# First loads, MLP entry and the end of the RWKV stage rearranged, RWKV preparation in fixed turns of two row halves

## The chip, the cores and the metric

The kernel runs on one core of one Trainium2 chip. The metric is the device time of one execution in microseconds (us). Three runs of the kernel before took 4267.73, 4275.2 and 4288.86 us, median 4275.2 us.

## The reference, cut to what matters

One inference step of a backbone of two layers on 1280 tokens (256 of a prompt, 1024 of a sample) of width 1024. Layer 0 mixes tokens with a gated DeltaNet beside a short convolution, layer 1 with windowed attention beside RWKV-7; each layer ends in an MLP of width 4096.

```python
for layer in range(2):
    mod = silu(c) @ mod_w[layer] + mod_b[layer]        # shift, scale, gate, twice; c_ctx for the prompt
    h = rmsnorm(x, norm_mix) * (1 + mod[1]) + mod[0]
    x = x + mod[2] * (even_mixer(h) if layer == 0 else odd_mixer(h))
    h = rmsnorm(x, norm_mlp) * (1 + mod[4]) + mod[3]
    x = x + mod[5] * (square(relu(h @ mlp_w1)) @ mlp_w2)
y = rmsnorm(x, norm_final)

def rwkv7_mixer(x):                                     # 8 heads of 64, both directions
    r, k, v, wl, al, gl = split(token_shift_bi(x, mu))
    decay = exp(-exp(-softplus(-(w0 + tanh(wl) @ w_up)) - 0.5))   # low rank 64, per direction
    a = sigmoid(a0 + al @ a_up)                                   # low rank 64, per direction
    kk = l2norm(k * k_k);  k2 = k * (1 + (a - 1) * k_a)
    y = scan(S = S*decay - (S kk)(kk*a)^T + v k2^T;  y = S r)     # forward + backward
    y = groupnorm(y) * ln_w + ln_b + sum(r * k2 * r_k) * v        # bonus
    return y * (sigmoid(gl) @ g_up)                               # gate
odd_mixer(h) = concat(attention(h), rwkv7_mixer(h)) @ w_out
```

## The kernel before, in words

Tokens stand along the free dimension and features on the 128 partitions: x is eight tiles of 128 x 1280. A dense product is exact to fp32 by three products of split operands (`split`, L245: hi = rounded copy on ACT, lo = src - hi on POOL or DVE; `dense_mm`, L270). The tokens are worked in chunks of 512, 512 and 256. A scheduler sets the order on each engine by a simulated time line; helpers steer it (`behind` and `late` put one instruction behind another, `chain` gives time to the serial work and `paced` spends it on dense work between).

Start (L1881 to L1898): x is loaded in five pieces of 1 MB on ACT's queue and transposed, the conditions c and c_ctx come on SP's queue (`load_vec(1)`, L196), two sets of modulation weights on SP's queue feed PE (`mod_set`, L297, products at L305), and the norm makes the first dense operands. `spill_x` (L124, store at L126) writes x out, 8 stores of 640 KB on SP's queue.

Even mixer (L590 on): `qkv(0, 1)`, then a product of 32 columns for beta and a (L711, L712), then `qkv(0, 0)`, `qkv(0, 2)`, `z_gate(0)`. Between the chunks `go_on(3)` issues three steps of the next modulation: ACT scales a weight tile (L357), POOL adds it up (L361). The squares of q and k are ACT's L630, their column sums PE's L635.

The first MLP starts behind a norm (L448, L455 on DVE). The modulation of layer 1 is made on DVE here (L348 and L350 in `mod_vec`), one step behind each eviction of the MLP's output (L512).

RWKV (L1298 on) runs in 8 units: 4 pairs of heads x 2 directions. A unit has five groups of 256 tokens, 40 groups in all. `prep` (L1524) makes a group's operands: two low-rank products (L1548) in one bank of `pp` (two banks), read by ACT (L1550); four Gram matmuls for each head (L1588), read by DVE (L1590); four transposes for each head (L1595), read by ACT (L1597). A head is a half of the 64 + 64 rows of the array. `recur` runs the serial chunks and alternates the halves matmul by matmul (L1698, L1713 and others). Dense products of the odd projection (L1276) and then attention fill PE between. `finish(b)` (L1797) ends a pair of heads after its second direction in five parts: load r and k (tile `vg`, one buffer), head norm, transposes L1827, bonus L1829, gate L1835, store to `sp_w` (L1838). For the first three pairs the parts run inside the next unit; for the last pair they run after unit 7.

`odd_out` (L1844): `unspill_x` loads x on ACT's queue in 24 pieces (L131); eight operands of 640 KB are loaded through two buffers on alternating queues (L1849) and split; `project` (L1861) multiplies them by od_w_out, 4 + 4 column blocks, and adds into x (L1866). Then come the norm, the second MLP and the final norm.

Of the kernel before, what the change touches and what calls it, by code (L numbers as in the profile page):

```python
# [85 lines left out]
def tile_kernel(ctx, tc, I, O):  # L86
# [37 lines left out]
    def spill_x(xt):  # L124
        for kb in range(KB):
            SY.dma_start(out=x_dram[kb], in_=xt[kb])  # L126
# [69 lines left out]
    load_vec(1, SY, const)  # L196

# [11 lines left out]
    def behind(bi, other):  # L209
        tc.add_manual_dep(bi.ins, other.ins.name, mybir.DependencyInfo(mybir.DependencyClass.NoSync, mybir.DependencyReason.DATA),  # L210
                          reason="one sum at a time in a bank")
# [77 lines left out]
    V.memset(scp, 0.0)  # L289
    for s, nm in enumerate(("c_ctx", "c")):  # L290
        th = cvec[:, s, :]
        A.activation(out=th, in_=vec[nm], func=AF.Tanh, scale=0.5)
        V.scalar_tensor_tensor(out=th, in0=th, scalar=1.0, in1=vec[nm], op0=ALU.add, op1=ALU.mult)
        V.tensor_scalar(out=scp[:, :, s], in0=th, scalar1=0.5, scalar2=None, op0=ALU.mult)
    mods = [const.tile([P, 48, 2], F32, name=f"mods{l}") for l in range(2)]

    def mod_set(wp, l, u):  # L297

        ps = ps_t("pm")
        for kb in range(KB):  # L300
            for j in range(2):
                w = wp.tile([P, 512], F32, tag="modw", name="modw")
                c0 = u * D + 512 * j
                SY.dma_start(out=w, in_=I["mod_w"][l, kb * P:(kb + 1) * P, c0:c0 + 512])
# [31 lines left out]
    def mod_vec(wp, ring, bank, l, c0, n, on_v, loads=None):  # L336
# [4 lines left out]
        for kb in range(KB):  # L341
            src = I["mod_w"][l, kb * P:(kb + 1) * P, c0:c0 + n]
            if on_v:
                w = state[ring].tile([P, n], F32, tag=ring, name="modw")
                SY.dma_start(out=w, in_=src)
                for s in range(2):
                    if kb == 0:
                        V.tensor_scalar(out=acc[:, s], in0=w, scalar1=scp[:, kb, s:s + 1], scalar2=None, op0=ALU.mult)  # L348
                    else:
                        V.scalar_tensor_tensor(out=acc[:, s], in0=w, scalar=scp[:, kb, s:s + 1], in1=acc[:, s],  # L350
                                               op0=ALU.mult, op1=ALU.add)
# [126 lines left out]
    def mlp(es, l, xt, hs, gate, side=()):  # L478
# [7 lines left out]
        for g in range(FF // 256):  # L486
# [16 lines left out]
            def down(hid, t0, N, s):  # L503
                hh, hl = hid
                for db in range(KB):
                    ps = ps_m()
                    for b in range(2):
# [4 lines left out]
                    V.scalar_tensor_tensor(out=xt[db][:, t0:t0 + N], in0=ps[:, :N],  # L512
                                           scalar=gate[:, db, s:s + 1], in1=xt[db][:, t0:t0 + N],
                                           op0=ALU.mult, op1=ALU.add)
# [66 lines left out]
    def even_mixer(hs):  # L581
# [9 lines left out]
        with ExitStack() as es:  # L591
# [19 lines left out]
            def qkv(h, i):  # L611
# [5 lines left out]
                for t0, N, s in CHUNKS:  # L617
# [4 lines left out]
                    go_on(3)  # L622
# [19 lines left out]
            def z_gate(j):  # L642
                hl = load_w(w_cols(wi, 1536 + j * P))
                zt_ = cp.tile([P, T], F32, tag="cv", name="zg", bufs=2)
                for t0, N, s in CHUNKS:
# [5 lines left out]
                    go_on(3)  # L651
# [4 lines left out]
            def short_conv(j, i):  # L656
# [5 lines left out]
                for t0, N, s in CHUNKS:  # L662
# [10 lines left out]
                    go_on(3)  # L673
# [18 lines left out]
            steps = mod_steps()  # L692
# [10 lines left out]
            hl = state["whl"].tile([P, KB, 2, 16], F32R, tag="whl", name="whl")  # L703
# [47 lines left out]
            for i in (0, 2):  # L751
                qkv(0, i)
# [324 lines left out]
    def odd_mixer(xt, hs, hes, xes, wes):  # L1077
# [20 lines left out]
        mid.update(a=sp_a, w=sp_w)  # L1098
# [53 lines left out]
        with ExitStack() as es:  # L1152
# [37 lines left out]
            for j in (12, 13, 14):  # L1190
# [9 lines left out]
                SY.dma_start(out=(sp_l[0], sp_l[1], sp_g)[j - 12], in_=dst)  # L1200
# [98 lines left out]
        with ExitStack() as es:  # L1299
# [22 lines left out]
            for u, (b, d) in enumerate(units):  # L1322
# [11 lines left out]
                else:  # L1334
# [4 lines left out]
                    if u >= 7:  # L1339
                        pace["used"] = max(pace["used"], start - 0)  # L1340
# [7 lines left out]
                if d == 1:  # L1348
                    ends = finish(b)
            for f in ends:  # L1350
                f()
# [148 lines left out]
    def rwkv(es, sp_r, sp_v, sp_t, sp_l, sp_g, sp_k2):  # L1500
# [23 lines left out]
        def prep(b, d):  # L1524
# [3 lines left out]
            if d == 0:  # L1528
                ups = tp.tile([P, 3, P], F32, tag="ups", name="ups", bufs=2)
                for i, src in enumerate((I["rwkv_w_up"].rearrange("e d r c -> (e d r) c"),  # L1530
                                         I["rwkv_a_up"].rearrange("e d r c -> (e d r) c"), I["rwkv_g_up"][0])):
                    SY.dma_start(out=ups[:, i], in_=src[:, b * P:(b + 1) * P])
# [5 lines left out]
            for c0 in order:  # L1538
# [4 lines left out]
                lin = tp.tile([P, 2, 256], F32, tag="lin", name="lin", bufs=1)  # L1543
                SY.dma_start(out=lin[hr[d]], in_=sp_l.rearrange("x p t -> p x t")[hr[d], :, sl])
                ps = ps_t("pp")
                lt = tp.tile([P, 2, 256], F32, tag="lt", name="lt", bufs=2)
                for i in range(2):
                    chain(PE.matmul(ps[:, 256 * i:256 * i + 256], ups[hr[d], i, :], lin[hr[d], i, :],  # L1548
                                    start=True, stop=True), 0.43)
                    A.activation(out=lt[:, i], in_=ps[:, 256 * i:256 * i + 256], func=AF.Tanh, scale=0.5,  # L1550
# [24 lines left out]
                g = state["more"] if state["more"] and turn[0] % 11 in (1, 2, 3) else gp  # L1575
# [9 lines left out]
                for h in range(2):  # L1585
                    ps = ps_t("pp")
                    for c in range(4):
                        chain(PE.matmul(ps[:, P * c:P * c + P], BK[hr[h], c, h:h + 2, :].rearrange("p a q -> p (a q)"),  # L1588
                                        AR[hr[h], c].rearrange("p a q -> p (a q)"), start=True, stop=True), 0.22)
                    V.tensor_tensor(out=Gm[:, :, h, 64:], in0=ps.rearrange("p (c q) -> p c q", c=4),  # L1590
                                    in1=gmask[:, d, h:h + 1].to_broadcast([P, 4, P]), op=ALU.mult)
                for h in range(2):
                    ps = ps_t("pp")
                    for c in range(4):
                        chain(PE.transpose(ps[:, 64 * c:64 * c + 64], BK[hr[h], c, h:h + 2, :].rearrange("p a q -> p (a q)"),  # L1595
# [362 lines left out]
```

## Time and profile before

| | us |
|---|---|
| median of three runs | 4275.2 |
| profiled execution | 4277.4 |
| its span | 4275.4 |
| PE busy (92%) | 3933.8 |
| DVE busy (53%) | 2285.1 |
| ACT / POOL busy (30% each) | 1285.4 / 1300.8 |
| mean granted TensorE clock | 0.944 |

The span is 1.9 us shorter than the profiled execution's own time. Busy time counts an engine's instructions, not its waits; the granted clock is the share of full TensorE speed (1.0 is 2.4 GHz, 0.5 is 1.2 GHz). In a waits view, "line <- engine tile line" is the instruction that waited and what ended the wait. In a timeline the bracket is the idle time ahead of an instruction and what ended it, and `x16` are sixteen records that stand as one row. A matmul of fp32 operands has two records.

### The profile page before, as it was taken

Reading aid. Unit: us, or ns where it says so; the run is one execution under the profiler, and the core shown is the slowest. Engines: PE = TensorE matmul, PEld = TensorE weight load, DVE = VectorE, ACT = ScalarE, POOL = GpSimd, SP = SyncE. Lnnn points to the kernel's source line nnn. Section 1 sums busy time; section 2 is a strip of 40 time slices with the busy share of each in tenths; the row PEclk is TensorE's granted clock in tenths of the full one; section 3 lists DMA queues with packets and bytes.
Section 4 is the critical chain, followed back from the end, with each engine's and each line's share of the span. In section 5 each row is a group of like instructions: output and inputs, shape, how many; then the busy total and the mean of one; then the engine's idle time right before and its main releaser. Section 6 shows DMA issues by size and latency. Waiting matters only on the chain. (4 is left out here: it accounts for less than half of the span.)

```text
span 4275.4 us, 68726 instructions
## 1 busy us (share of the span) xinstructions
PE 3933.8 (92%) x27295; PEld 3228.1 (76%) x27295; DVE 2285.1 (53%) x4799; ACT 1285.4 (30%) x2721; POOL 1300.8 (30%) x1139
## 2 busy tenths in 40 slices
PE   6889989998999999999889889999868899999999
PEld 3677877786888888877667667777647788888887
DVE  5377676546455555463365577778541533333335
ACT  4454543223111111143222234444321311111112
POOL 2444542224222332242432231212022323322232
PEclk8889999999999999999989889999879999999999
DMA  5323332332122222125466543333242111111111
GB/s 206 101 81 100 93 98 70 126 131 73 53 75 72 71 79 75 47 98 181 147 211 185 137 101 82 91 88 82 64 134 67 30 40 40 40 35 35 40 40 60
DMA packets 437952, 382.90 MB, mean 90 GB/s; under 512 B 125684, under 2 KB 373503, under 8 KB 437503
## 3 DMA queue, kind: packets, MB, share of 16 engines
q1 hardware_dynamic: 405802, 314.45, 25.0%
q10 hardware_dynamic: 31829, 64.06, 4.5%
q8 instruction: 215, 3.52, 0.3%
q14 instruction: 106, 0.87, 0.1%
HBM read 290.31 MB, written 88.08 MB: 89 GB/s over the span
## 5 line engine op out<-in xcount | busy, mean ns | idle before, releaser
L275 PE MATMUL pd<-hhi,whl 128*128 128x512 f32 (+1 forms) x5376 | 1538.8, 366 | 55.0 <-ACT hhi L247 25.3
L275 PEld LDWEIGHTS pd<-hhi,whl 128*128 128x128 f32 x5376 | 974.9, 193 | 213.4 <-ACT hhi L247 27.1
L275 PE MATMUL pd<-hlo,whl 128*128 128x512 f32 (+1 forms) x2688 | 986.0, 367 | 27.1 <-POOL hlo L251 13.4
L512 DVE SCALAR_TENSOR_TENSOR x<-pm,mods,x 128x512 f32<-128x512 f32 (+1 forms) x768 | 501.7, 659 | 724.9 <-PE pm L511 724.7
L251 POOL TENSOR_TENSOR whl<-raw,whl 128x1024 fp32r<-128x1024 f32 (+1 forms) x203 | 471.2, 2331 | 611.3 <-ACT whl L247 610.1
L275 PEld LDWEIGHTS pd<-hlo,whl 128*128 128x128 f32 x2688 | 518.1, 193 | 115.3 <-DVE hlo L455 19.2
L509 PE MATMUL pm<-hh,whl 128*128 128x512 f32 (+1 forms) x1536 | 545.7, 356 | 0.0
L510 PE MATMUL pm<-hl,whl 128*128 128x512 f32 (+1 forms) x1536 | 544.4, 354 | 0.0
L511 PE MATMUL pm<-hh,whl 128*128 128x512 f32 (+1 forms) x1536 | 542.9, 354 | 0.0
L498 ACT ACTIVATE t<-pd 128x512 f32<-128x512 f32 (+1 forms) x192 | 101.1, 528 | 1307.6 <-PE pd L275 1305.3
L251 POOL TENSOR_TENSOR hl<-t,hh 128x512 fp32r<-128x512 f32 (+1 forms) x192 | 217.6, 1134 | 822.5 <-DVE hh L249 802.5
L509 PEld LDWEIGHTS pm<-hh,whl 128*128 128x128 f32 x1536 | 288.9, 188 | 44.5
L510 PEld LDWEIGHTS pm<-hl,whl 128*128 128x128 f32 x1536 | 289.4, 188 | 43.5
L511 PEld LDWEIGHTS pm<-hh,whl 128*128 128x128 f32 x1536 | 289.5, 188 | 41.7
L249 DVE CAST hh<-t 128x512 fp32r<-128x512 f32 (+1 forms) x192 | 164.0, 855 | 228.4 <-ACT t L499 228.3
L247 ACT ACTIVATE whl<-raw 128x1024 fp32r<-128x1024 f32 (+1 forms) x203 | 201.7, 1011 | 162.8 <-PE pm L511 74.7
L361 POOL TENSOR_TENSOR acc<-acc,modw 128x512 f32<-128x512 f32 x112 | 152.3, 1360 | 151.9 <-ACT modw L357 132.4
L357 ACT ACTIVATE modw<-modw,scp 128x256 f32<-128x256 f32 x224 | 113.0, 506 | 67.3 <-DMA modw<-in_mod_w_dram 61.9
L1276 PE MATMUL pa<-hst,whl 128*128 128x512 f32 (+1 forms) x432 | 121.1, 380 | 9.5 <-DMA hst<-sp_h 8.5
L350 DVE SCALAR_TENSOR_TENSOR acc<-modw,scp,acc 128x512 f32<-128x512 f32 x168 | 129.1, 800 | 0.2 <-DMA modw<-in_mod_w_dram 0.2
L284 PE MATMUL pd<-hhi,whl 128*128 128x512 f32 (+1 forms) x384 | 109.2, 364 | 4.9 <-ACT hhi L247 3.0
L420 ACT ACTIVATE sq<-x 128x512 f32<-128x512 f32 (+1 forms) x120 | 66.2, 558 | 157.3 <-DVE x L1866 48.0
(388 smaller groups left out, 5989.8 us busy)
## 6 DMA issues: line engine op xcount, KB each, us to landing
raw<-in_mlp_w_dram SPq DMA_DIRECT2D x128, 512.0 KB
modw<-in_mod_w_dram SPq DMA_DIRECT2D x128, 256.0 KB
hst<-sp_h ACTq DMA_DIRECT2D x48, 512.0 KB
modw<-in_mod_w_dram SPq DMA_DIRECT2D x128, 128.0 KB
rkk<-sp_r SPq DMA_DIRECT2D x40, 384.0 KB
raw<-in_ev_w_in_dram SPq DMA_DIRECT2D x28, 512.0 KB
x_dram<-x SPq DMA_DIRECT2D x16, 640.0 KB
x<-x_dram ACTq DMA_DIRECT2D x32, 256.0 KB
```

The source lines that it names most:

```text
L247: A.activation(out=hi, in_=src, func=AF.Copy)
L249: V.tensor_copy(out=hi, in_=src)
L251: G.tensor_tensor(out=lo, in0=src, in1=hi.bitcast(F32), op=ALU.subtract)
L275: paced(PE.matmul(ps[:, :N], w, x[:, t0:t0 + N], start=(n + i == 0), stop=(n == KB - 1 and i == 2)), N / 2400)
L350: V.scalar_tensor_tensor(out=acc[:, s], in0=w, scalar=scp[:, kb, s:s + 1], in1=acc[:, s], op0=ALU.mult, op1=ALU.add)
L357: bi = A.activation(out=dst[:, s], in_=w[:, 0], func=AF.Copy, scale=scp[:, kb, s:s + 1])
L361: G.tensor_tensor(out=acc, in0=acc, in1=w, op=ALU.add)
L509: PE.matmul(ps[:, :N], wh, hh[:, b, :N], start=(b == 0), stop=False)
L510: PE.matmul(ps[:, :N], wh, hl[:, b, :N], start=False, stop=False)
L511: PE.matmul(ps[:, :N], wl, hh[:, b, :N], start=False, stop=(b == 1))
L512: V.scalar_tensor_tensor(out=xt[db][:, t0:t0 + N], in0=ps[:, :N], scalar=gate[:, db, s:s + 1], in1=xt[db][:, t0:t0 + N], op0=ALU.mult, op1 ...
L1276: burst([(lambda w_=w_, i=i, w=w, h=h: PE.matmul(st["ps"][w_][:, :N], st["w"][w_][:, w, kb, :], x[:, h, :N], start=(kb + i == 0), stop=(kb ...
```

## The change

1. Start: the conditions are loaded on ACT's queue after the first two pieces of x (`conditions()`), the modulation weights come first on SP's queue, and the eight stores of x stand behind the last of them. 2. Even mixer: `qkv(0, 1)` and `qkv(0, 0)` come ahead of the beta and a product, which has tiles of its own; `go_on` begins at the tenth call with four steps each. 3. First MLP: DVE's modulation steps stand behind an eviction of the MLP's output. 4. RWKV preparation: the low-rank inputs of w and a of one direction are stored on opposite partition halves; the two low-rank products, the eight transposes and the eight Gram matmuls of a group each run as one fixed run that alternates the row halves and writes two banks; the transposes come ahead of the Gram matmuls; the times given to `chain` are lower. 5. RWKV's end: bonus and gate of the last pair of heads are made inside unit 7 (`ahead`) and stored; after the chain remain norm, transposes, one multiply-add, sum, product, store (`rest`). 6. `odd_out`: operands are loaded straight into the lo tiles and split in place, in the order 0, 1, 2, 4, 5, 6, 3, then x[7], then operand 7 in three pieces, then x[6] to x[0]; `project` takes the operands in that order.

```diff
@@ start
-    load_vec(1, SY, const)
+    def conditions():
+        load_vec(1, A, const)
         ...
         load_x(xp_, xt, (2, 4))
+        conditions()
         ...
-        spill_x(xt)
+        spill_x(xt, state["last"])
@@ even mixer
-            def go_on(n):
-                for _ in range(n):
-                    next(steps, None)
-            qkv(0, 1)
-            raw = state["raw"].tile([P, KB, 16], F32, tag="raw", name="raw")
+            def go_on():
+                if next(calls) >= 9:
+                    for _ in range(4):
+                        next(steps, None)
+            for i in (1, 0):
+                qkv(0, i)
+            raw = ge.tile([P, KB, 16], F32, tag="D1", name="rawb", bufs=1)
@@ first MLP, mod_vec
+                    late(bi, state["evict"])
@@ RWKV prep
-                lin = tp.tile([P, 2, 256], F32, tag="lin", name="lin", bufs=1)
-                SY.dma_start(out=lin[hr[d]], in_=sp_l.rearrange("x p t -> p x t")[hr[d], :, sl])
-                ps = ps_t("pp")
+                lin = tp.tile([P, 256], F32, tag="lin", name="lin", bufs=2)
+                SY.dma_start(out=lin, in_=sp_l[d][:, sl])
+                pss = [ps_t("pp"), ps_t("pp")]
+                run_of([lambda i=i, q=q: PE.matmul(pss[i][:, :256], ups[q, i, :], lin[q, :], start=True, stop=True)
+                        for i, q in enumerate((hr[d], hr[1 - d]))], 0.22)
         ...
+                pss = [ps_t("pp"), ps_t("pp")]
+                run_of([lambda c=c, h=h: PE.transpose(pss[h][:, 64 * c:64 * c + 64], both(c, h), ident[hr[h], hr[h]])
+                        for c in range(4) for h in (1, 0)], 0.07)
         ...
+                psg = [ps_t("pp"), ps_t("pp")]
+                run_of([lambda c=c, h=h: PE.matmul(psg[h][:, P * c:P * c + P], both(c, h),
+                                                   AR[hr[h], c].rearrange("p a q -> p (a q)"), start=True, stop=True)
+                        for c in range(4) for h in (1, 0)], 0.11)
+    def run_of(calls, us):
+        last = None
+        for f in calls:
+            if last is None:
+                bi = f()
+            else:
+                with tc.high_priority():
+                    bi = f()
+                behind(bi, last)
+            chain(bi, us)
+            last = bi
@@ RWKV end
+                if u == 7:
+                    pre, last = finish(b)
+                    slot = [f for k, f in enumerate(slot) for f in ([f, pre.pop(0)] if k % 4 == 3 and pre else [f])] + pre
         ...
+            def rest(c0):
+                ...
+                SY.dma_start(out=eg[:, 0:2], in_=mid["e"][:, :, sl])
+                head_norm(Yt)
+                ps = ps_t("pa")
+                by_feature(ps, Yt)
+                affine(eg[:, 2], ps)
+                G.tensor_tensor(out=eg[:, 2], in0=eg[:, 2], in1=eg[:, 0], op=ALU.add)
+                V.tensor_tensor(out=eg[:, 2], in0=eg[:, 2], in1=eg[:, 1], op=ALU.mult)
+                SY.dma_start(out=mid["w"][b][:, sl], in_=eg[:, 2])
@@ odd_out
-                a = gp.tile([P, T], F32, tag="a", name="a", bufs=2)
-                (SY if j % 2 else A).dma_start(out=a, in_=mid["a"][j] if j < 4 else mid["w"][j - 4])
-                split(hs[j][0], hs[j][1], a, "a", "v" if j % 2 else "g")
+                dma = SY.dma_start(out=lo.bitcast(F32), in_=(mid["a"][j] if j < 4 else mid["w"][j - 4])[:, sl])
+                split(hi, lo, lo.bitcast(F32), "a", eng_lo)
         ...
-    unspill_x(xt)
     odd_out(xt, hs, mod_gate(1, 0))
```

How the order on the engines moves, at three places. On SP, at the program's start, before (`modw` are modulation weights, `raw` dense weights, `x_dram` the spilled x):

```order
L304 DMA modw<-in_mod_w_dram 128x512 x17
L263 DMA raw<-in_ev_w_in_dram 128x8x128
L702 DMA raw<-in_ev_w_in_dram 128x8x16
L304 DMA modw<-in_mod_w_dram 128x512 x8
L126 DMA x_dram<-x 128x1280 x3
L304 DMA modw<-in_mod_w_dram 128x512 x2
L126 DMA x_dram<-x 128x1280 x4
L304 DMA modw<-in_mod_w_dram 128x512 x4
L126 DMA x_dram<-x 128x1280
L304 DMA modw<-in_mod_w_dram 128x512
L263 DMA raw<-in_ev_w_in_dram 128x8x128 x2
```

The same place on SP, now:

```order
L321 DMA modw<-in_mod_w_dram 128x512 x11
L276 DMA raw<-in_ev_w_in_dram 128x8x128 x2
L321 DMA modw<-in_mod_w_dram 128x512 x10
L276 DMA raw<-in_ev_w_in_dram 128x8x128
L321 DMA modw<-in_mod_w_dram 128x512 x2
L276 DMA raw<-in_ev_w_in_dram 128x8x128
L321 DMA modw<-in_mod_w_dram 128x512 x9
L126 DMA x_dram<-x 128x1280 x8
L722 DMA rawb<-in_ev_w_in_dram 128x8x16
```

All eight stores of x moved behind the last of the 32 modulation tiles, and the four weight loads stand ahead of them.

On PE, the first group of the RWKV preparation, before (`pp` are its banks; L1276 is a dense product, `pi` the serial work's bank):

```order
L1548 MATMUL pp<-lin,ups 128x256
L1276 MATMUL pa<-hst,whl 128x512 x3
L1548 MATMUL pp<-lin,ups 128x256
L1276 MATMUL pa<-hst,whl 128x512 x3
L1641 MATMUL pi<-cst,sraw 64x64 x2
L1276 MATMUL pa<-hst,whl 128x512 x6
L1657 MATMUL pi<-cst,AR 64x64 x2
L1588 MATMUL pp<-AR,BK 128x128 x4
L1276 MATMUL pa<-hst,whl 128x512 x6
L1588 MATMUL pp<-AR,BK 128x128 x4
L1276 MATMUL po<-hst,whl 128x512 x2
L1595 MATMUL pp<-cst,BK 128x64 x4
```

The same group on PE, now:

```order
L1577 MATMUL pp<-lin,ups 128x256 x2
L1302 MATMUL pa<-hst,whl 128x512 x3
L1672 MATMUL pi<-cst,sraw 64x64 x2
L1302 MATMUL pa<-hst,whl 128x512 x2
L1688 MATMUL pi<-cst,AR 64x64 x2
L1618 MATMUL pp<-cst,BK 128x64 x8
L1302 MATMUL pa<-hst,whl 128x512 x7
L1623 MATMUL pp<-AR,BK 128x128 x8
```

The single products and runs of four became runs of two and eight, the transposes (L1618) moved ahead of the Gram matmuls (L1623), and dense products still stand between the runs.

On SP, from the last stores of the RWKV stage to the operands of the odd output projection, before (`vg` holds a part's inputs, `a` an operand):

```order
L1806 DMA vg<-sp_r 128x256
L1806 DMA vg<-sp_k_16314 128x256
L1838 DMA sp_w<-yT 128x256
L1806 DMA vg<-sp_k_16314 128x256
L1823 DMA vg<-sp_g 128x256
L1822 DMA vg<-sp_v 128x256
L1838 DMA sp_w<-yT 128x256
L1849 DMA a<-sp_a 128x1280
L1849 DMA a<-sp_w 128x1280 x2
```

The same place on SP, now (`eg` holds a part's bonus, gate and result, `hlo` the operand's lo tile):

```order
L1915 DMA sp_w<-eg 128x256
L276 DMA raw<-in_od_w_out_dram 128x4x128
L1929 DMA hlo<-sp_a 128x1280 x3
L1929 DMA hlo<-sp_w 128x1280 x3
L1929 DMA hlo<-sp_a 128x1280
L1935 DMA x<-x_dram 128x1280
L1929 DMA hlo<-sp_w 128x512
L1929 DMA hlo<-sp_w 128x256
L1929 DMA hlo<-sp_w 128x512
L1940 DMA x<-x_dram 128x1280 x7
```

The loads of a part's inputs are gone from the end, all operand loads moved to SP without a buffer between them, and x comes behind them instead of ahead of them on ACT's queue.

## Rows read from the trace of the kernel before

**Rows 1.** Page of the profile: engine totals, then granted TensorE clock in 40 slices (tenths).

```profile
PE 3933.8 (92%) x27295; PEld 3228.1 (76%) x27295; DVE 2285.1 (53%) x4799; ACT 1285.4 (30%) x2721; POOL 1300.8 (30%) x1139
...
PEclk8889999999999999999989889999879999999999
```

**Rows 2.** Windows: stretch, its length, busy time of each engine, granted clock, DMA share, GB/s.

```profile
0.00:66.00 66.00, 41.33 (x186) 20.28 (x186) 20.37 (x52) 20.50 (x49) 12.19 (x15) 0.90 0.90 322
...
960.00:1008.00 48.00, 30.30 (x143) 23.76 (x142) 45.16 (x66) 25.03 (x44) 29.45 (x16) 0.83 0.39 121
...
2260.00:3080.00 820.00, 742.81 (x9028) 571.90 (x9026) 574.91 (x1603) 316.59 (x824) 185.70 (x268) 0.90 0.39 103
...
3140.00:3190.00 50.00, 25.15 (x266) 17.87 (x262) 17.47 (x44) 6.43 (x12) 17.05 (x19) 0.62 0.50 156
3190.00:3235.00 45.00, 22.00 (x72) 16.64 (x72) 9.86 (x5) 9.94 (x8) 11.60 (x4) 0.70 0.50 168
3235.00:3335.00 100.00, 99.55 (x514) 83.97 (x512) 20.37 (x33) 16.24 (x22) 20.50 (x11) 1.00 0.13 37
```

**Rows 3.** Transfers of the first 70 us: issues with count and size of one.

```profile
x_dram<-x SPq DMA_DIRECT2D x8, 640.0 KB
```

**Rows 4.** What PE waited for in the first 150 us: sum, times, longest.

```profile
PE pm L635 <- ACT t L630: 13.3, 2, 12.7
```

**Rows 5.** Timeline of PE at 69 us: start, duration, line, operation, wait before it.

```profile
69.36 0.79 PE L275 MATMUL pd<-hhi,whl 128*128 128x512 f32 x1 [2.01 <-ACT hhi L454]
```

**Rows 6.** Timeline of ACT, 112 to 118 us.

```profile
112.18 1.05 ACT L357 ACTIVATE modw<-modw,scp 128x256 f32<-128x256 f32 x2 [4.84 <-DMA modw<-in_mod_w_dram]
...
117.76 0.61 ACT L630 ACTIVATE t<-cv 128x512 f32<-128x512 f32 x1
```

**Rows 7.** Groups of DVE by line, 960 to 1008 us: count, busy us, mean ns.

```profile
L350 DVE SCALAR_TENSOR_TENSOR acc<-modw,scp,acc 128x512 f32<-128x512 f32 x14 | 12.3, 887 | 0.0
```

**Rows 8.** PE by line and form, 2100 to 3200 us: count, busy us, mean ns.

```profile
L1588 PE MATMUL pp<-AR,BK 64*128 64x128 f32 x640 | 83.3, 308 | 15.6 <-DVE BK L1580 12.9 <-DVE BK L1581 1.0 <-DVE rn L1140 1.0
L1548 PE MATMUL pp<-lin,ups 64*128 64x256 f32 x160 | 61.1, 465 | 15.0 <-DMA lin<-sp_l 13.4 <-ACT Gm L1597 0.9 <-ACT lt L1550 0.6
```

**Rows 9.** Timeline of PE, runs of one row half, 2532 to 2539 us.

```profile
2532.05 1.71 PE L1588 MATMUL pp<-AR,BK 64*128 64x128 f32 x16
...
2536.35 0.46 PE L1595 MATMUL pp<-cst,BK 64*128 64x64 f32 x4
...
2538.93 0.70 PE L1548 MATMUL pp<-lin,ups 64*128 64x256 f32 x2
```

**Rows 10.** Timeline of PE, runs of alternating halves, 3121 to 3126 us.

```profile
3121.16 1.04 PE L1698 MATMUL pi<-AG,Gm 64*64 64x128 f32 x16
...
3125.97 0.68 PE L1675 MATMUL pi<-t,Gm 64*64 64x64 f32 x16
```

**Rows 11.** The banks pp, 2260 to 3080 us: their readers, ns min/median/max.

```profile
L1597 ACT ACTIVATE Gm<-pp x65: 375/384/393, 2260.5 to 2993.6; 128x256 f32<-128x256 f32 x65
L1550 ACT ACTIVATE lt<-pp,hv x64: 450/474/492, 2261.0 to 2973.5; 128x256 f32<-128x256 f32 x64
L1590 DVE TENSOR_TENSOR Gm<-pp,gmask x64: 672/681/694, 2305.1 to 2982.7; 128x512 f32<-128x512 f32 x64
```

**Rows 12.** What PE waited for, 2100 to 2260 us.

```profile
PE pp L1548 <- DMA lin<-sp_l: 13.4, 1, 13.4
```

**Rows 13.** Timeline of PE, ACT and POOL, 3176 to 3202 us.

```profile
3176.11 1.12 PE L1827 MATMUL pa<-cst,Yt 64*64 64x64 f32 x16 [2.87 <-POOL Yt L1818]
...
3183.64 15.86 ACTq L131 DMA_DIRECT2D x<-x_dram  x24
...
3199.54 2.43 ACT L247 ACTIVATE hhi<-a 128x1280 fp32r<-128x1280 f32 x2 [16.98 <-DMA x<-x_dram]
...
3200.86 1.43 PE L275 MATMUL pd<-hhi,whl 128*128 128x512 f32 x3 [17.26 <-ACT hhi L247]
3200.89 2.89 POOL L251 TENSOR_TENSOR hlo<-a,hhi 128x1280 fp32r<-128x1280 f32 x1 [16.69 <-ACT hhi L247]
```

More of the change, by code (lines that the diff above doesn't have):

```diff
@@ L122, in tile_kernel, with spill_x @@
     x_dram = dram.tile([KB, P, T], F32, name="x_dram")
-    def spill_x(xt):
+    def spill_x(xt, after=None):
         for kb in range(KB):
-            SY.dma_start(out=x_dram[kb], in_=xt[kb])
+            dma = SY.dma_start(out=x_dram[kb], in_=xt[kb])
+            if after is not None:
+                late(dma, after)
     def unspill_x(xt):
@@ L210, in behind @@
         tc.add_manual_dep(bi.ins, other.ins.name, mybir.DependencyInfo(mybir.DependencyClass.NoSync, mybir.DependencyReason.DATA),
-                          reason="one sum at a time in a bank")
+                          reason="in order")
     def burst(calls, size):
@@ L288, in tile_kernel @@
     cvec = const.tile([P, 2, KB], F32, name="cvec")
[L289 to L294, printed above, removed]
+    def conditions():
+        load_vec(1, A, const)
+        V.memset(scp, 0.0)
+        for s, nm in enumerate(("c_ctx", "c")):
+            th = cvec[:, s, :]
+            A.activation(out=th, in_=vec[nm], func=AF.Tanh, scale=0.5)
+            V.scalar_tensor_tensor(out=th, in0=th, scalar=1.0, in1=vec[nm], op0=ALU.add, op1=ALU.mult)
+            V.tensor_scalar(out=scp[:, :, s], in0=th, scalar1=0.5, scalar2=None, op0=ALU.mult)
     mods = [const.tile([P, 48, 2], F32, name=f"mods{l}") for l in range(2)]
@@ L749, in even_mixer @@
             V.tensor_scalar(out=negc, in0=ex[:, :, 0], scalar1=-1.0, scalar2=None, op0=ALU.mult)
-            for i in (0, 2):
-                qkv(0, i)
+            qkv(0, 2)
             z_gate(0)
@@ L1199, in odd_mixer @@
                     V.tensor_scalar(out=dst, in0=dst, scalar1=0.5, scalar2=0.5, op0=ALU.mult, op1=ALU.add)
-                SY.dma_start(out=(sp_l[0], sp_l[1], sp_g)[j - 12], in_=dst)
+                if j == 14:
+                    SY.dma_start(out=sp_g, in_=dst)
+                else:
+                    for d in range(2):
+                        o = d if j == 12 else 1 - d
+                        SY.dma_start(out=sp_l[d, 64 * o:64 * o + 64], in_=dst[64 * d:64 * d + 64])
             for w_ in range(3):
@@ L1347, in odd_mixer @@
                     ends.pop(0)()
-                if d == 1:
+                if d == 1 and b < 3:
                     ends = finish(b)
-            for f in ends:
+            for f in last:
                 f()
@@ L1574, in prep @@
                     turn[0] += 1
-                g = state["more"] if state["more"] and turn[0] % 11 in (1, 2, 3) else gp
+                g = state["more"] if state["more"] and turn[0] % 11 in (9, 10, 0) else gp
                 AR = g.tile([P, 4, 2, 64], F32, tag="AR", name="AR")
@@ L1845, in odd_out, with operand @@
         with ExitStack() as e2:
-            gp = pool(e2, "odo", 2)
-            for j in range(KB):
-                a = gp.tile([P, T], F32, tag="a", name="a", bufs=2)
-                (SY if j % 2 else A).dma_start(out=a, in_=mid["a"][j] if j < 4 else mid["w"][j - 4])
-                split(hs[j][0], hs[j][1], a, "a", "v" if j % 2 else "g")
+            def operand(j, sl, eng_lo):
+                hi, lo = hs[j][0][:, sl], hs[j][1][:, sl]
+                dma = SY.dma_start(out=lo.bitcast(F32), in_=(mid["a"][j] if j < 4 else mid["w"][j - 4])[:, sl])
+                split(hi, lo, lo.bitcast(F32), "a", eng_lo)
+                return dma
+            for j in (0, 1, 2, 4, 5, 6, 3):
+                last = operand(j, slice(0, T), "v" if j in (2, 5) else "g")
+            first = SY.dma_start(out=xt[7], in_=x_dram[7])
+            late(first, last)
+            for t0, N, s in (CHUNKS[1], CHUNKS[2], CHUNKS[0]):
+                last = operand(7, slice(t0, t0 + N), "v")
+            for kb in range(KB - 2, -1, -1):
+                late(SY.dma_start(out=xt[kb], in_=x_dram[kb]), last)
             w = I["od_w_out"][0]
```

120 lines of the change are left out of this document (72 added, 48 removed).

## The prediction

> **What bounds the kernel now.** I read the engine totals first: PE is busy for 3933.8 of 4275.4 us, and its clock is at full speed in most of the 40 slices [rows 1]. DVE, ACT and POOL have room on the average, so an edit pays where it removes work from PE, time in which PE waits, or time at the half clock (1.2 GHz). The windows say where these are [rows 2]. In the first 66 us the DMA engines are 90% busy at 322 GB/s and PE for 41.33 us: the loads set the pace. At the first MLP's entry, 960 to 1008, PE is busy for 30.30 of 48 us while DVE is busy for 45.16. In the long RWKV stretch, 2260 to 3080, PE is busy for 742.81 of 820 us at a mean clock of 0.90. From 3140 to 3190 it has 25.15 of 50 us at 0.62, and to 3235 another 22.00 of 45 us at 0.70: there PE waits for the end of a serial chain and for loads, not for itself. After that it runs full, 99.55 of 100 us at 1.00. The waits view and the timelines then give the single waits below.
>
> The sum is made against the profiled execution, 4277.4 us, which is 2.2 us above the median of 4275.2 us; I take 2.2 us off at the end.
>
> **Start.** Eight stores of 640 KB [rows 3] stand on SP between the modulation loads; the change puts them behind all of these. They are 5.24 MB, at the stretch's 322 GB/s [rows 2] 16.3 us of a full DMA. The first dense product starts at 69.36 us [rows 5]; what it needs is all of x and of these weights. Not all the stores are issued ahead of the last weight in time to hold it, so I take -13 us, between 0 (the loads of x are late instead, since now the weights start beside them) and -16. The stores still have to go out, beside the first dense products, whose four weight tiles are now ahead of them; nothing else large is due there. The conditions move behind ACT's first instructions, which can delay the first modulation product; PE has a third of this stretch free to catch up, so I add nothing.
>
> **Even mixer's entry.** PE's longest wait of the first 150 us is 12.7 of 13.3 us, for the squares on ACT (L630) [rows 4]. ACT stood behind modulation weights: its scalings waited 4.84 us for a load and the square ran only at 117.76 [rows 6]. Now `qkv(0, 0)` follows at once, ahead of the small product, and no step is issued by the first nine calls; the scheduler still leaves a few scalings between, but with a dense product behind PE's wait rather than a product of 32 columns. I take the wait off, 12.7, and some 1.5 us of the half clock behind it: -14 us. The bounds are 0 (the wait moves to PE's next reader of ACT) and -25 (the clock after it recovers as well). Four steps a call instead of three, later, can make ACT wait for weights elsewhere: one such wait is 4.84 us [rows 6], hidden unless an eviction stands behind it. I take 0, with 8 us to either side.
>
> **First MLP's entry.** Fourteen L350 steps take 12.3 us of DVE's time in the midst of the norm [rows 7], and PE is idle for 17.7 of these 48 us [rows 2]. They move behind evictions of the MLP's output, where DVE has room (53% over the span [rows 1]). Half of the norm's work is on ACT and POOL, so not all of it shortens: -9 us, between 0 and -13.
>
> **RWKV preparation.** The 640 records of L1588 [rows 8] are 16 for each of 40 groups. A run of 16 in one row half takes 1.71 us at full clock [rows 9]; a run of 16 of the same 128 columns that alternates the halves, with no wait, takes 1.04 us [rows 10]: 0.67 us a group. A low-rank product by itself takes 0.70 us [rows 9], of which the last record's 0.27 us or so (1.04 and 0.68 are alike in that tail) overlaps what follows; the second of a pair in turns hides behind the first, 0.43 us a group. Four transposes take 0.46 us [rows 9]; the alternating run of 64 columns has 16 records in 0.68 us [rows 10], which says that here too there is something, and I take 0.10 us. That is 1.2 us x 40 = 48 us of PE's time.
>
> The tiles are a kind the Trainium skill speaks of: "TensorEngine Tiling (Array Packing)", Theoretical Speedup, gives up to 2 times where a dimension is at most 64. By it the Gram run would fall to 0.86 us, the saving would be 8 us larger over 40 groups and the forecast, at the half taken below, 4 us lower; the trace's own pair of runs, 1.71 against 1.04, shows 1.64 times, and the measurement decides.
>
> Does PE's time there reach the end? PE is busy for 91% of the stretch, so most of it should; but its idle 77 us are waits of the serial chain for DVE and ACT, which don't shrink, and dense work runs out sooner. The clock speaks too: between 91% busy at 0.90 and 50% busy at 0.62 [rows 2] the slope is 0.28 / 0.40 = 0.7, so 48 us less in 820 (6%) could cost 0.04 of clock, which on 742.81 us is about +35 us. I take half the saving, -24 us, with bounds of -48 and +35. The order shows other work between transposes and Gram matmuls in nearly all groups, so the banks' evictions have cover. The single wait of 13.4 us for `lin` at the stretch's entry [rows 12] is the first load after the projections; it stays, 0, at best -13.
>
> **RWKV's end and the odd output.** The last transposes of the chain run at 3176.11 [rows 13]; then the last part still loads its inputs, and only when its store is away can ACT's queue issue 24 loads of x, 15.86 us long. ACT's first split starts at 3199.54 after 16.98 us, PE's first product at 3200.86 after 17.26 us. By 3235 72 of 576 products (8 blocks x 24 x 3 chunks) are done [rows 2]; the other 504 fill the next 99.6 us or so, 14.2 us a block. So the work itself is 8 x 14.2 = 113.6 us, and it ends at 3334.6.
>
> Now, after 3176.11 there are a transposition of 1.1 us, an affine, a sum and a product of some 0.5 us each, and a store: the operand loads can start at about 3180. SP has one weight load ahead of them. Seven operands of 655 KB are 4.6 MB, 14 us at 322 GB/s; x[7] and operand 7 add 4 us: 3198, and 3 to 4 us for the splits and the last products of the first block, so 3202. POOL's lo tiles, five of 2.89 us [rows 13], are 14.5 us in the same time and don't come later. Seven blocks follow: 3202 + 99.4 = 3301, a gain of 33 us. At best the loads are hidden whole, 3180 + 113.6 = 3294: -41. At worst the loads are as late as before and only ACT's 15.86 us go: -15. The bonus and gate of the last pair move into unit 7, where PE has 9% free.
>
> **Sum.** -13 - 14 - 9 - 24 - 33 = -93 us; 4277.4 - 93 - 2.2 = 4182 us. All low ends together give about 4111, all high ends 4303.
>
> **Rivals.**
> 1. The preparation's saving reaches the end in full (for: 91% busy; against: the chain's own waits): 24 us more, 4158 us.
> 2. It doesn't reach it, because the chain of DVE and ACT sets the pace there, or because the halves don't overlap after all and the change doesn't do what it says: a Gram run would still show 1.71 us. 24 us less, 4206 us.
> 3. The operands are late all the same (their tiles' memory is still in use when SP comes to them, or POOL's splits queue up): the end gains 15 instead of 33 us, 4200 us.
> 4. Slower: each fixed run takes both `pp` banks, so the next run waits for both evictions. Two of L1550 at 0.474, two of L1597 at 0.384 and two of L1590 at 0.681 us [rows 11] are 3.1 us a group, 123 us over 40 groups where PE has nothing between. With the other gains (-69) that is +54, 4329 us. It decides from 1.7 us a group on (69 / 40), and passes 0.5% from 2.25 us. Against it: the order has a median of 25 matmuls between transposes and Gram matmuls, and before, too, each bank was waited for (0.9 and 0.6 us in L1548's row [rows 8]).
>
> The Trainium skill names the fourth as a pattern: "TensorEngine Tiling (Array Packing)", PSUM Bottleneck, says that tiling speeds up TensorE but not the evacuation of PSUM, which may become the bottleneck. The trace of before has the two about level, 1.04 us of matmuls to 1.36 us of evictions in a Gram run, and no run yet shows which ends last.
>
> **How the numbers follow.** The forecast with half the saving 0.42 (its own range 4155 to 4215), rival 1 0.16, rival 2 0.20, rival 3 0.14, rival 4 0.08. The range of 4115 to 4250 leaves out rival 4 and the far ends of the start's and the end's bounds. About 0.5% (21 us) is what a measurement of this kernel can tell from no change: slower by more than that is most of rival 4, 0.05; within it the rest of rival 4 and cases in which two or three terms fall to their high ends, 0.07; faster 0.88.
>
> **What would show it.** Right: the first dense product near 56 us; no wait of 12.7 us at the column sums; PE's idle time at the MLP's entry near 9 us; Gram runs of 16 records in some 1.05 us at full clock; PE's first product of the odd output near 3183 less the earlier gains, then 14 us a block. Wrong: the clock of the RWKV stretch under 0.86, waits of `pp` matmuls for L1597's and L1590's successors of over 1 us a group, or an odd output that waits for its operands until 20 us after the last transposes.

## The result and the profile after

The changed kernel took 4235.0 us (median of 4 runs, 4222.59 to 4237.1), the kernel before 4279.9 us beside it: ratio 0.9895, 95% interval 0.9869 to 0.9921. It is 45 us faster; 93 were forecast, and 4235 is within the range. Its profiled span is 4232.3 us, 43.1 less than before.

The page's engine totals, in answer to [rows 1]:

```profile
PE 3871.4 (91%) x27295; PEld 3182.1 (75%) x27295; DVE 2288.5 (54%) x4800; ACT 1283.3 (30%) x2728; POOL 1309.4 (31%) x1140
```

PE is busy for 62.4 us less, though the time fell by 43. To see where, I cut both traces at the same events (first dense product; last result of the even mixer in x; first and last second product of the first MLP; first low-rank product; last transposes of RWKV's chain; last result of the odd output):

| stage, us | before | after | difference | forecast |
|---|---|---|---|---|
| start | 69.4 | 68.9 | -0.4 | -13 |
| even mixer | 902.1 | 889.7 | -12.4 | -14 |
| first MLP's entry | 44.1 | 32.3 | -11.8 | -9 |
| first MLP, norm, odd projections | 1097.9 | 1093.5 | -4.4 | 0 |
| RWKV stretch | 1063.7 | 1076.5 | +12.8 | -24 |
| RWKV's end and odd output | 158.0 | 131.1 | -26.9 | -33 |
| second MLP and end | 940.2 | 940.3 | +0.1 | 0 |

The windows of the changed kernel answer to [rows 2]: entry of the first MLP, entry of the RWKV stretch, the whole stretch, then the odd output.

```profile
958.60:990.90 32.30, 28.31 (x107) 21.76 (x107) 24.01 (x36) 17.89 (x34) 20.09 (x15) 0.80 0.25 74
2084.40:2220.40 136.00, 89.61 (x532) 67.50 (x533) 76.72 (x151) 37.21 (x84) 61.02 (x67) 0.74 0.60 175
2084.40:3160.90 1076.50, 894.99 (x10762) 685.00 (x10762) 697.77 (x1907) 387.44 (x1007) 267.38 (x360) 0.88 0.43 116
...
3172.00:3192.00 20.00, 17.15 (x72) 13.58 (x72) 15.64 (x7) 9.18 (x9) 17.09 (x5) 0.80 1.02 412
3192.00:3292.00 100.00, 99.48 (x514) 84.01 (x512) 20.44 (x33) 16.57 (x23) 20.48 (x11) 1.00 0.14 42
```

The two windows of the stretch in the kernel before:

```profile
2113.50:2249.50 136.00, 118.41 (x612) 85.94 (x612) 78.09 (x158) 39.32 (x86) 50.33 (x67) 0.87 0.71 211
2113.50:3177.20 1063.70, 947.92 (x10758) 725.51 (x10758) 702.40 (x1905) 388.31 (x1002) 256.84 (x359) 0.89 0.43 117
```

At the first MLP's entry PE is idle for 4.0 us (32.30 - 28.31), before for 15.0 of the 44.1 us. In the stretch PE is busy for 52.9 us less, somewhat more than the 48 forecast, and is not busy for 181.5 instead of 115.8 us: what was saved came back as idle time, and more. At the entry PE issues 532 records instead of 612 in the same 136 us, and its clock is at 0.74 instead of 0.87.

In the even mixer, the wait of PE's column sums for the squares on ACT, in answer to [rows 4]:

```profile
PE pm L653 <- ACT t L648: 2.4, 1, 2.4
```

PE's timeline of the runs, at full clock, in answer to [rows 9]:

```profile
2597.97 0.46 PE L1618 MATMUL pp<-cst,BK 64*128 64x64 f32 x8
2599.81 1.16 PE L1623 MATMUL pp<-AR,BK 64*128 64x128 f32 x16
2603.57 0.70 PE L1577 MATMUL pp<-lin,ups 64*128 64x256 f32 x4
```

A Gram run takes 1.16 us (1.71 before), and two low-rank products take as long as one did (0.70 us): there the halves overlap, though no run has such a pair in one half to compare. Eight transposes take 0.46 us, as long as four did, but that isn't the halves: without alternation eight in one run take 0.47 us (experiment below). What they gain is that they stand together. The lines of the stretch answer to [rows 8]: Gram, low-rank and transposes are busy for 55.2, 43.0 and 21.2 us, before for 83.3, 61.1 and 36.6.

```profile
L1623 PE MATMUL pp<-AR,BK 64*128 64x128 f32 x640 | 55.2, 311 | 1.1 <-ACT Gm L1621 0.9 <-POOL AR L1608 0.2
...
L1577 PE MATMUL pp<-lin,ups 64*128 64x256 f32 x160 | 43.0, 460 | 24.9 <-DMA lin<-sp_l 13.8 <-DVE Gm L1627 9.4 <-DMA ups<-in_rwkv_w_up_dram 1.6
```

Waits for the evictions of the two banks are 9.4 and 0.9 us over 40 groups, 0.26 us a group, far from the 1.7 at which the fourth rival decides.

The start, in answer to [rows 5]: the timeline of PE, then SP's longest wait and ACT's last issue of x.

```profile
26.97 7.34 PE L322 MATMUL pm<-modw,scp 128*32 128x512 f32 x20 [8.66 <-DVE scp L310]
...
68.91 0.80 PE L288 MATMUL pd<-hhi,whl 128*128 128x512 f32 x1 [2.01 <-ACT hhi L472]
```

```profile
SPq L321 <- DMA raw<-in_ev_w_in_dram: 12.0, 1, 12.0
```

```profile
38.16 0.40 ACTq L482 DMA_DIRECT2D xs<-in_x_prompt_dram  x1
```

The modulation products begin at 26.97 us instead of 16.79, since the conditions (`scp`) come late. The last piece of x, whose buffer is freed by transposes queued on PE behind those products, is issued at 38.16 us instead of 25.59. PE's windows from the first to the last modulation product, now and then before, with a wait that the kernel before has and the changed one hasn't:

```profile
26.97:64.80 37.83, 34.40 (x152) 14.73 (x152) 13.64 (x32) 13.93 (x31) 11.42 (x9) 0.95 0.86 307
```

```profile
16.79:65.00 48.21, 34.24 (x152) 14.04 (x152) 15.39 (x35) 16.04 (x39) 11.98 (x11) 0.86 0.97 351
...
PE pm L305 <- DMA modw<-in_mod_w_dram: 8.4, 3, 5.4
```

The new order of the loads did its work: PE no longer waits for modulation weights, and the same 34 us of PE's work takes 37.8 instead of 48.2 us. But it begins 10.2 us later and is 91% busy, so it ends where it ended before. SP's wait of 12.0 us is put down by the view to the dense weight load `raw`, issued at 16.77 and landed at 29.40; no modulation product waited for a weight because of it.

At the end, in answer to [rows 13]: PE, ACT and SP after the last transposes.

```profile
3159.80 1.12 PE L1861 MATMUL pa<-cst,Yt 64*64 64x64 f32 x16 [6.31 <-POOL Yt L1856]
...
3165.96 1.29 SPq L1929 DMA_DIRECT2D hlo<-sp_a  x3
...
3170.28 1.27 ACT L260 ACTIVATE hhi<-hlo 128x1280 fp32r<-128x1280 f32 x1 [8.76 <-DMA hlo<-sp_a]
3171.61 1.43 PE L288 MATMUL pd<-hhi,whl 128*128 128x512 f32 x3 [10.69 <-ACT hhi L260]
```

PE's gap is 10.69 instead of 17.26 us, and the first 72 products are done 31 us after the last transposes instead of 58.

### The profile page after: what moved, and what is told of

It reads as the page before. It is cut to its first block, busy times and chain, and to the rows that moved or that the text cites. A ratio compares the mean times of both kernels' runs of the same rounds, so it can differ in the third digit from the quotient of the medians.

```text
span 4232.3 us, 68874 instructions
## 1 busy us (share of the span) xinstructions
PE 3871.4 (91%) x27295; PEld 3182.1 (75%) x27295; DVE 2288.5 (54%) x4800; ACT 1283.3 (30%) x2728; POOL 1309.4 (31%) x1140
## 5 line engine op out<-in xcount | busy, mean ns | idle before, releaser
L262 DVE CAST hh<-t 128x512 fp32r<-128x512 f32 (+1 forms) x192 | 134.2, 700 | 198.2 <-ACT t L517 198.2
L367 DVE SCALAR_TENSOR_TENSOR acc<-modw,scp,acc 128x512 f32<-128x512 f32 x168 | 163.0, 970 | 0.0
```

Of the source, the lines that this page charges most:

```text
L262: V.tensor_copy(out=hi, in_=src)
L367: bi = V.scalar_tensor_tensor(out=acc[:, s], in0=w, scalar=scp[:, kb, s:s + 1], in1=acc[:, s], op0=ALU.mult, op1=ALU.add)
```

## The experiments

Three rounds each; the time is the median of the timed runs, the ratio is against the kernel before, run beside it. Its medians there were 4277.4 us (the first four experiments), 4275.8 (the next four) and 4272.3 (the last four), and 4279.9 beside the changed kernel, so a few us between two experiments say little. "Stretch" is the RWKV stage of the table, read from one profile of each kernel.

**Old values for the pacing.**

```diff
-                        for i, q in enumerate((hr[d], hr[1 - d]))], 0.22)
+                        for i, q in enumerate((hr[d], hr[1 - d]))], 0.43)
-                        for c in range(4) for h in (1, 0)], 0.07)
+                        for c in range(4) for h in (1, 0)], 0.13)
-                        for c in range(4) for h in (1, 0)], 0.11)
+                        for c in range(4) for h in (1, 0)], 0.22)
```

> The changed kernel with only the times that the preparation's runs report to the pacing put back to the old sizes (0.43, 0.13, 0.22 us instead of 0.22, 0.07, 0.11). In the changed kernel the RWKV stretch, first low-rank product to last transposes of the chain, takes 1076.5 us with PE idle for 181.5 us, before 1063.7 us with 115.8 us idle. Theory A (the lowered values halve the dense work that is granted to the first preparation, so PE idles at the entry and the saved PE time is lost): the first 136 us of the stretch come back from 89 to about 118 us of PE busy time, the stretch falls to 1030 to 1050 us, the kernel to about 4195 to 4210 us. Rival B (the fixed runs in two banks make PE wait for evictions and operands): the stretch stays at 1070 to 1080 us, the time at 4230 to 4240 us.

4193.8 us, ratio 0.9814 (0.9794 to 0.9834), stretch 1033.3 us: theory A by its numbers, but for the entry's busy time, 109 us instead of 118. The matmuls are the same; some 41 us hung on what they report to the pacing.

**Preparation as before.** The edit puts back the lines under "RWKV prep" in the diff above, with the layout and the turns.

> The changed kernel with the whole preparation of the RWKV stage put back (layout of the low-rank inputs, order, banks, times given to the pacing, turns of the extra buffers); all other parts stay. Theories A and B (the loss is in the preparation): the stretch from the first low-rank product to the last transposes is 1064 us or less, the kernel at about 4222 us. Rival C (the loss comes from bonus and gate of the last pair of heads moved into unit 7): the stretch stays near 1076 us and the last transposes come no earlier, 4235 us or, without the saved PE time, 4260 us and more.

4217.4 us (0.9868, 0.9844 to 0.9891), stretch 1053.5 us: theories A and B, the loss is in the preparation, and rival C is out. By the medians the preparation as it was changed cost 18 us, and with the old values it gives 24 (4217.4 - 4193.8).

**Conditions on SP's queue.**

```diff
+    load_vec(1, SY, const)
     ...
     def conditions():
-        load_vec(1, A, const)
```

> The changed kernel with the conditions loaded at the program's start on SP's queue again; the stores of x stay behind the modulation weights. Theory D (on ACT's queue the conditions come late: scp at 26.97 us instead of 16.79, the 11 buffers of the modulation weights are full, SP stands for 12 us and the last piece of x is issued at 38 instead of 26 us, which eats what the moved stores gave): the modulation products start near 17 us, SP's 12 us wait is gone, the first dense product comes near 57 us instead of 68.9, the kernel at about 4223 us. Rival E (the first loads are bound by something else, the same bytes in another order): first dense product at 66 to 69 us, 4235 us.

4255.3 us (0.9957, 0.9940 to 0.9974): slower than the changed kernel. The start behaves as theory D says, products from 17.43 and first dense product at 60.46 us (57 was expected), but the even mixer takes 904.8 us instead of 889.7 and the stretch 1085.9. So earlier conditions do bring the first dense product forward, and the theory's sum doesn't hold.

**No alternation.**

```diff
-                        for c in range(4) for h in (1, 0)], 0.11)
+                        for h in (1, 0) for c in range(4)], 0.11)
```

and the same for the transposes.

> The changed kernel with the same fixed runs, banks and times, but the transposes and Gram matmuls of one head all ahead of those of the other, so that row halves don't alternate. If the alternation makes halves overlap, Gram runs of 16 records take 1.7 us at full clock here against 1.1 us in the changed kernel and PE is busy for 25 to 35 us more. Theory A or B (PE's time in the stretch isn't what sets the end): the time changes by less than 10 us. Rival F (PE's time does set it, and another loss of some 60 us hides the gain): the time rises by 25 to 45 us, to 4260 to 4280 us.

4279.4 us (1.0002, 0.9987 to 1.0018), stretch 1127.8 us: rival F, 44 us. Gram runs take 1.71 us again, eight transposes 0.47 us:

```profile
2530.55 0.47 PE L1618 MATMUL pp<-cst,BK 64*128 64x64 f32 x8
2547.20 1.71 PE L1623 MATMUL pp<-AR,BK 64*128 64x128 f32 x16
```

So the alternation acts on the Gram runs alone. PE is busy for 61 us more in the stretch, where 25 to 35 were expected; the Gram line gives 33 of them (88.6 instead of 55.2). PE's time in the stretch does reach the end.

**First grant alone.**

```diff
-            grant["ratio"] = 4
+            grant["ratio"] = 7.8
```

> The changed kernel with one number altered: the share of dense work granted per reported us during the first unit's preparation is 7.8 instead of 4 (4 x 3.66 / 1.88, the ratio of the old and new sums of a group), the lowered values themselves stay. Theory A1 (the loss is the entry alone: dense products missing in the first unit, pushed into later units): stretch 1030 to 1040 us as in the kernel with the old values (1033.3), time about 4195 us. Rival A2 (the lowered values also place the work badly within the later units): the entry's busy time comes back to 110 us of 136, but the stretch falls only by some 25 us to about 1050 us, time about 4210 us.

4193.6 us (0.9805, 0.9787 to 0.9822), stretch 1034.4 us: theory A1. One number, in force for the preparation of the first unit alone, gives back as much as the old values do. Its windows, entry and whole stretch:

```profile
2075.90:2211.90 136.00, 108.30 (x621) 79.57 (x622) 80.28 (x165) 39.56 (x89) 54.65 (x70) 0.84 0.70 212
...
2075.90:3110.30 1034.40, 877.84 (x10762) 668.48 (x10762) 698.33 (x1907) 388.70 (x1007) 258.61 (x360) 0.92 0.44 121
```

Against the changed kernel's stretch PE is not busy for 156.6 instead of 181.5 us (25 us), and the same work takes 17 us less busy time at a clock of 0.92 instead of 0.88: 42 us. The loss doesn't show at the entry itself. Of the chain's 144 updates of the state, counted from the first low-rank product, the 64th starts at 588 us in the changed kernel, at 601 us here; the 127th at 1001 against 958. The last dense product of the projection starts at 364 us there, at 288 here. So the dense work left out early was paid for later; which waits it makes there isn't shown.

**Old values and conditions on SP together.** The two edits above.

> The changed kernel with the old values for the pacing and the conditions on SP's queue. If the start's gain of 8 us holds and the loss of 15 us in the even mixer of the kernel with the conditions alone was an accident of the new order: 4180 to 4188 us, below the old values alone (4194). Rival (an earlier start always costs the even mixer as much, since its first loads come in behind the stores of x): even mixer again near 905 us from first dense product to its last result, time 4200 us or more.

4223.2 us (0.9869, 0.9849 to 0.9889); even mixer 902.9, stretch 1057.0 us: the rival's numbers; its reason isn't shown.

**First MLP's entry as before.**

```diff
-                    late(bi, state["evict"])
```

> The changed kernel without the one line that puts DVE's modulation steps of the first MLP behind an eviction. If the entry's gain (last result of the even mixer to first second product of the MLP, 44.1 us before, 32.3 now) comes from these steps: 42 to 45 us again, time +8 to +13, 4243 to 4248 us. Rival (the gain comes from the norm's other work, as the whole order moved): 32 to 35 us, time unchanged at 4235 us.

4270.9 us (0.9988, 0.9978 to 0.9997). The entry takes 43.5 us again, as expected; the remaining 25 us are not explained by it: the stretch, whose code is the same, takes 1097.0 us in another order, 20 more.

**Even mixer's order as before.** The edit puts back the lines under "even mixer" in the diff above.

> The changed kernel with the even mixer's order before: small product behind qkv(0, 1), three modulation steps for each call from the first call on. If the wait of the column sums for ACT (12.7 us before, 2.4 now) comes from that order: a wait of 8 to 15 us at the column sums again, even mixer 900 us instead of 889.7, time 4243 to 4250 us. Rival (the late start of the modulation loads alone, behind the stores, removed it): the wait stays under 4 us, time 4230 to 4240 us.

4254.9 us (0.9946, 0.9931 to 0.9961). The wait of the column sums is there again, and the even mixer takes 896.6 us:

```profile
PE pm L653 <- ACT t L648: 13.3, 2, 12.7
```

Again more is lost than that: the stretch takes 1090.8 us.

**Kernel before with the low values.**

```diff
-                                    start=True, stop=True), 0.43)
+                                    start=True, stop=True), 0.22)
```

and 0.11 for 0.22, 0.07 for 0.13.

> The kernel before with the lowered values alone (0.22, 0.11, 0.07 us reported by the preparation instead of 0.43, 0.22, 0.13), its matmuls as they are. Theory A (the values set how much dense work the first unit gets, and that costs by itself): PE's busy time in the first 136 us of the stretch falls from 119 to about 90 us, the stretch grows from 1063.7 to 1095 to 1110 us, the kernel to about 4310 us. Rival (the low values hurt only together with the runs in two banks): 1055 to 1075 us, 4270 to 4285 us.

4341.5 us (1.0165, 1.0150 to 1.0180), 69 us slower with not one matmul changed; stretch 1127.3 us, entry 108 us busy at 0.73. The values cost by themselves, more than expected, though the entry's busy time falls less than the expected 119 to 90 us: 522 records instead of 612, at the lower clock.

**First grant, no alternation.** The two edits above.

> The kernel with the first grant at 7.8 (4193.6 us, stretch 1034.4), but one head's transposes and Gram matmuls ahead of the other's. If the overlap of the halves is worth the same where the pacing is right (the two effects add): stretch 1075 to 1085 us, time 4235 to 4245 us. Rival (half of the 51 us between the kernels with and without alternation was the order's accident or the bad pacing): stretch 1050 to 1065 us, time 4212 to 4225 us.

4216.5 us (0.9872, 0.9856 to 0.9889), stretch 1056.9 us: the rival. In the well paced kernel the alternation is worth 23 us by this pair; the other half of the 44 belonged to the bad pacing or to the order's accident, which isn't told apart, and the order alone can move the stretch by as much (below).

**First grant, end as before.** Parts 5 and 6 of the change are put back.

> The kernel with the first grant at 7.8, with RWKV's end and the odd output as in the kernel before (all parts of the last pair behind the chain, x loaded first on ACT's queue, operands through two buffers). If the rearranged end is worth what the stages say (158.0 before, 131.1 now from the last transposes to the last result): 155 to 160 us again, time 4217 to 4225 us. Rival (the move of bonus and gate into unit 7 costs the stretch some of it): the stretch falls by 5 to 10 us at the same time, time 4210 to 4215 us.

4214.4 us (0.9863, 0.9848 to 0.9877); from the last transposes to the last result 162.3 instead of 131.3 us, and the stretch 1029.3 instead of 1034.4: the end gives 31 us, as expected. The stretch falls by 5 us as the rival says, but a difference of that size is within what another order makes, so it isn't shown that the work moved into unit 7 costs it.

**First grant, conditions first on ACT's queue.**

```diff
+        conditions()
         load_x(xp_, xt, (2, 4))
-        conditions()
```

> The kernel with the first grant at 7.8, with the conditions first on ACT's queue, ahead of the first pieces of x. Theory D (the conditions came late): modulation products start 8 to 10 us earlier than at 27 us, SP's wait behind the full buffers is 2 to 4 us instead of 12, first dense product at 56 to 60 us against 65.6. If the even mixer keeps its 888 us the kernel takes about 4187 us; if it loses 15 us again, as both kernels with the conditions on SP did, about 4200 us.

4205.5 us (0.9843, 0.9825 to 0.9862). The modulation products start at 23.47 us, only 2.5 us earlier than without this edit, where 8 to 10 were expected. The start still falls to 60.4 us, the even mixer rises to 907.1 and the stretch, whose code is the same, from 1034.4 to 1046.7. PE's order in the even mixer (5420 records) is the same, record for record, in the changed kernel and in five others with its start and its even mixer, and takes 885 to 891 us there; the three kernels with an early start have other orders and take 903 to 907. Why the scheduler's order is worse there, or whether some of it is the stores of x, stays open.

## Why the prediction was wrong, point by point

- **Start: wrong, -0.4 instead of -13.** The step that failed: "PE has a third of this stretch free to catch up, so I add nothing". The free time lies ahead of the conditions, where PE stood for 8.66 us, and can't be used behind them: from 26.97 us on PE is busy for 34.4 of 37.8 us. So the new order of the loads gave 10.4 us (48.2 to 37.8) and the late conditions took 10.2. The three kernels with early conditions start their dense products at 60.4 to 61.9 us, against 65.6 to 69.2 in the nine that have the change's start; their even mixer took it back. The best of them is 9 us below the kernel before, so the 13 weren't reached in any.
- **Even mixer's entry: right**, -12.4 for -14. The wait of 12.7 us is 2.4 now, and comes back whole with the old order, which costs the stage 6.9 us.
- **First MLP's entry: right**, -11.8 for -9; it comes back without the one line.
- **RWKV preparation: wrong, +12.8 instead of -24.** The saving on PE was sized low, 48 us for 61.6 in the three lines: the low-rank term fits (0.45 us a group for 0.43), the Gram runs gave 0.70 for 0.67, and the transposes 0.39 for 0.10, by standing in one run and not by the halves. The half that reaches the end came out too, 24 us where the old values are kept; as the stretch differs by as much without any change to it (1033.3 and 1057.0 us in the two kernels with the old values), this may be luck. What failed is that the values given to `chain` had no term at all. I took them for a description of the runs; they are the currency in which dense work is released. By the kernel's own reckoning the first unit is granted 5 groups x (3.66 - 1.88) us x 4 = 35.6 us less of dense products. In the traces 378 instead of 558 of the 648 dense products start ahead of the first unit's first `fin` product (L1823; L1792 in the kernel before); with the first grant at 7.8 they are 549. In five pairs of kernels that differ in the pacing alone, the stretch is longer by 29 to 71 us with the small grant, by 42 and 43 for the changed kernel. That is more than the 9 to 24 us by which the stretch differs between kernels with the same code and pacing for it.
- **The clock's part of the bound isn't borne out.** The +35 rested on a slope of the clock over PE's busy share. The share of the stretch fell from 0.89 to 0.83 and the clock only from 0.89 to 0.88, and two kernels with a share of 0.85 had clocks of 0.86 (no alternation) and 0.92 (first grant at 7.8). The result lies within the bound by the pacing and not by this reason. Rival 2's outcome came about without either of its reasons: Gram runs do overlap, and PE's time does reach the end. (Of the 77 us that I called waits for DVE and ACT, 14 are waits for loads.)
- **The fourth rival is refuted**: 0.26 us of waits a group. The Trainium skill's sentence on the evacuation of PSUM ("TensorEngine Tiling (Array Packing)", PSUM Bottleneck), which it gives for a fourfold speedup, found no case here. A Gram run is faster by 1.47 times, 1.71 to 1.16 us, below the 1.64 that I read from a run of 64 x 64 tiles. The Trainium skill's factor of up to 2 (the same title, Theoretical Speedup) isn't reached; what I called 8 us by it is 7 (40 x 0.18).
- **RWKV's end and odd output: right in mechanism**, -26.9 for -33, and 31 us are lost by undoing it. The first operand load is issued at 3165.96, 5 us after the transposes instead of 3, and the operands' first block takes 31 us instead of 25; the blocks then take 14 us as worked out.

The sum: 12.6 us are missing at the start and 36.8 us in the RWKV stretch. The best kernel found is the changed one with the first grant at 7.8: 4193.6 us.

## What to carry to other kernels

When an edit makes an operation faster, look for every place where its duration is written down as a number: a pacing or a planner's budget fed by it changes too, and must be re-tuned with it. When a load moves to another queue, add up all the work that stands behind its reader on that engine: idle time ahead of a late input is no room for what comes behind it. And where a scheduler writes the order, undo a part only with a table by stages beside the total: the total mixes the part with orders that the edit didn't mean.

## What the runs showed that I had not expected

- Work granted too late shows first as a lead: the chain was 13 us ahead at the 64th update, and 43 us behind at the 127th.
- The same source lines in another order are worth as much as a part of this change: the RWKV stretch took 1076.5, 1085.9, 1090.8 and 1097.0 us in four kernels with the same code for it, 1033.3 and 1057.0 in the two with the old values, 1034.4 and 1046.7 in two with the first grant at 7.8. Each is one profile, and the runs of one kernel spread over 5 to 20 us, so part of these differences can be that.
- Two low-rank products of 256 columns on opposite row halves take 0.70 us, as long as one. Eight transposes of 64 columns take 0.46 us in turns and 0.47 without, as long as a run of four by itself: here alternation gives nothing, and joining the runs does.
